# 128 more bytes of spare line between the split weights and everything allocated behind them

## The chip, the cores and the metric

The kernel runs on one core of a Trainium2 chip. The metric is the device time of one execution in microseconds, median over the runs. One execution was also recorded by the profiler; its trace gives the start and duration of every instruction.

## The reference

A two-layer decoder trunk over 256 tokens of width 1024, in float32, batch 1. Layer 0 mixes with a gated linear recurrence and stick-breaking attention, layer 1 with a diagonal state-space model (S5) and a causal softmax attention; each layer has a SwiGLU feed-forward part with 2816 hidden units. Cut to what matters here:

```python
for layer in range(2):
    h = rms_norm(x, g)
    x = x + mixer(h)                    # one input projection, two branches, one output projection
    h = rms_norm(x, g2)
    x = x + (silu(h @ w_gate) * (h @ w_up)) @ w_down
return rms_norm(x, g3)
```

Nearly all of the arithmetic is `activations @ weights` with 1024 x 1024-like float32 matrices, 186 pieces of 512 KB in all.

## The kernel before, in words

Activations stay on the chip, transposed: feature on the 128 partitions, 256 tokens along the free axis. `x` holds the residual stream as 8 blocks of 128 x 256. All weights come from one array `wall`, in the order in which they are used, as 186 pieces of 128 x 1024 floats (8 blocks of 128 x 128 each).

Every float32 operand of a large product is split in two parts that TensorE reads in its one-pass format for 4-byte numbers (float32r): a rounded high part and the rest. A weight piece arrives in a tile `raw`; ScalarE writes `hi` (a copy rounded to float32r, line 109) and VectorE writes `lo = raw - hi` (line 112 or 114). An activation is split in the same way into `xh`, `xl` (and `hh`, `hl` in the feed-forward part, `yh`, `yl`, `ah`, `al`, `syh`, `syl` in the mixers). Each 128 x 128 block of weights then costs three matmuls into the same PSUM tile: hi with xh, hi with xl, lo with xh. This is line 160 (`dense`) and line 169 (`dense2`, which alternates between two outputs). The weights are the stationary operand, 128 columns, loaded anew for every matmul; the activations are the moving operand, 256 columns streamed through the array. There is one other form, line 368 (`proj_v`): the activations are stationary there, and the weights move, 512 columns per matmul. The stick-breaking attention has 16 float32r matmuls of its own (line 463, moving `sph`/`spl`, stationary `tr_r`).

Pieces are loaded up to six ahead and split up to three ahead of their use, through pools of four `raw` tiles and of five `hi` and five `lo` tiles. The order on TensorE and on the DMA queue is the order of the program text; the other engines are ordered by a scheduler.

The pools of a partition's memory are laid out one behind the other in the order in which they are opened (lines 70 to 79). A small helper puts spare space between two of them: `half_line(name)` opens a pool that holds one tile of 16 floats, 64 bytes, per unit of `n`; nothing reads or writes that tile.

```python
70  def half_line(name, es=ctx, n=1):
71      es.enter_context(tc.tile_pool(name="line_" + name, bufs=1)).tile([128, 16 * n], F32, name="line_" + name)
    ...
73  rawp = ctx.enter_context(tc.tile_pool(name="raw", bufs=LOAD_AHEAD - SPLIT_AHEAD + 1))
74  half_line("a")
75  wp = ctx.enter_context(tc.tile_pool(name="wp", bufs=SPLIT_AHEAD + 2))
76  half_line("b")
77  xp = ctx.enter_context(tc.tile_pool(name="xp", bufs=1))
    ...
160 PE.matmul(ps, lhsT=w, rhs=a, start=(j == 0 and i == 0), stop=(j == n - 1 and i == 2))
    ...
368 PE.matmul(o, lhsT=a[:, k, xs], rhs=w, start=(k == 0 and i == 0), stop=(k == 7 and i == 2))
```

In the built program the `raw` tiles start at byte 24000 of a partition and at steps of 4096 from there (192 modulo 256), the `hi` and `lo` tiles at 40448 and at steps of 4096 (0 modulo 256), `x`, `xh` and `xl` at 81472, 89664 and 97856 (64 modulo 256). The blocks inside a tile begin at multiples of 512 bytes, so this remainder holds for each of them. Further half lines keep `yh`, `yl`, `ah`, `al`, `hh`, `hl`, `syh` and `syl` at 64 modulo 256 too. So at lines 160 and 169 the moving operand always starts 64 bytes above the stationary one, modulo 256; at line 368, where the two change places, it starts 64 bytes below; at line 463, where both lie behind the weights, the two remainders are equal.

Of the kernel before, what the change touches and what calls it, by code (L numbers as in the profile page):

```python
# [49 lines left out]
def trunk_kernel(  # L50
# [19 lines left out]
    def half_line(name, es=ctx, n=1):  # L70
        es.enter_context(tc.tile_pool(name="line_" + name, bufs=1)).tile([128, 16 * n], F32, name="line_" + name)
# [1 line left out]
    rawp = ctx.enter_context(tc.tile_pool(name="raw", bufs=LOAD_AHEAD - SPLIT_AHEAD + 1))  # L73
    half_line("a")
    wp = ctx.enter_context(tc.tile_pool(name="wp", bufs=SPLIT_AHEAD + 2))
    half_line("b")
    xp = ctx.enter_context(tc.tile_pool(name="xp", bufs=1))
    rp = ctx.enter_context(tc.tile_pool(name="rp", bufs=2))
    half_line("r")
# [1175 lines left out]
```

## Time and profile before

| | us |
|---|---|
| median of 3 runs | 608.91 |
| lowest, highest | 607.36, 609.07 |
| the profiled execution, as timed | 608.91 |
| its span, first to last instruction | 607.1 |
| TensorE busy | 591.0 |
| VectorE busy | 438.4 |
| ScalarE busy | 346.2 |
| GpSimd busy | 208.3 |

The profiled execution's time equals the median, and lies 1.8 us above its span. In the trace a matmul's record begins when its operands start to stream and ends when its last result is written, so records of successive matmuls overlap, and busy time says little about pace: the pace of TensorE is the distance between the starts of two successive matmuls. A weight load has records of its own (PEld), which run beside the matmul before it. Engines are called PE (TensorE), DVE (VectorE), ACT (ScalarE), POOL (GpSimd) and SP (the queue that issues most DMAs).

### The profile page before, as it was taken

How to read it: one execution, taken by the hardware profiler on the slowest of the kernel's cores; microseconds unless marked ns; L12 is line 12 of the kernel's file. 1: busy time of each engine (PE TensorE's matmuls, PEld its weight loads, DVE VectorE, ACT ScalarE, POOL GpSimd, SP SyncE). 2: the span in 40 equal slices, each digit the busy share in tenths (PEclk: the TensorE clock that was granted, in tenths of full speed). 3: DMA queues.
4: the chain of work that ended last, by engine and by line, in shares of the span. 5: the costliest groups of instructions: out<-in, count | busy, mean ns of one | idle time of the engine just before them, and what ended most of it. 6: DMA issues, size and time to landing. Idle time of an engine off the chain costs nothing.

```text
span 607.1 us, 11926 instructions
## 1 busy us (share of the span) xinstructions
PE 591.0 (97%) x4840; PEld 576.0 (95%) x4840; DVE 438.4 (72%) x636; ACT 346.2 (57%) x480; POOL 208.3 (34%) x203
## 2 busy tenths in 40 slices
PE   8899999999999999999999999999999999999995
PEld 7799889999899999999999998899999999999994
DVE  5798998896999976637857992797756655556632
ACT  6769996942443535465656268766545434344452
POOL 0810001539999999159810000022121110021131
PEclk9999999999999999999999999999999999999998
DMA  8746345753465774536544422455555555655501
GB/s 314 257 155 194 108 161 183 243 153 128 144 198 181 240 226 156 174 105 201 181 162 128 143 91 70 167 177 189 177 194 177 189 190 181 201 174 186 196 1 70
DMA packets 29319, 102.76 MB, mean 169 GB/s; under 512 B 3520, under 2 KB 3536, under 8 KB 29264
## 3 DMA queue, kind: packets, MB, share of 16 engines
q1 hardware_dynamic: 28080, 99.36, 50.0%
q10 hardware_dynamic: 864, 1.57, 0.7%
q0 software_dynamic: 320, 1.06, 0.5%
q8 instruction: 38, 0.62, 0.4%
q14 instruction: 17, 0.14, 0.1%
HBM read 100.93 MB, written 1.05 MB: 168 GB/s over the span
## 4 chain that ended last, share of the span: by engine, by line
PE 73%; DVE 12%; ACT 6%; POOL 3%; issue 3%; DMA 2%; SPq 0%; DVEq 0%; POOLq 0%; ACTq 0%
PE mm L160 64%; DVE lo L112 3%; PE mm L169 3%; ACT u L907 1%; ACT hi L109 1%; DMA raw<-wall 1%; DMA x<-xT 1%; PE ax L169 1%; PE ax L780 1%; POOL acc L217 1%; PE mm L903 1%; PE ax L852 1%; ACT s5tt L785 1%; POOL s5st L715 1%; PE ax L260 1%
## 5 line engine op out<-in xcount | busy, mean ns | idle before, releaser
L112 DVE TENSOR_TENSOR lo<-raw,hi 128x1024 fp32r<-128x1024 f32 x184 | 245.2, 1339 | 95.4 <-ACT hi L109 95.2
L109 ACT ACTIVATE hi<-raw 128x1024 fp32r<-128x1024 f32 (+1 forms) x188 | 195.2, 1048 | 179.7 <-PE mm L160 104.9
L160 PE MATMUL mm<-xh,hi 128*128 128x256 f32 x896 | 254.6, 284 | 0.8 <-ACT xh L943 0.7
L160 PE MATMUL mm<-xh,lo 128*128 128x256 f32 x896 | 250.5, 280 | 2.2 <-DVE lo L112 2.2
L160 PE MATMUL mm<-xl,hi 128*128 128x256 f32 x896 | 250.6, 280 | 0.2
L160 PEld LDWEIGHTS mm<-xh,lo 128*128 128x128 f32 x896 | 167.8, 187 | 3.0 <-DVE lo L112 3.0
L160 PEld LDWEIGHTS mm<-xh,hi 128*128 128x128 f32 x896 | 168.4, 188 | 1.7 <-ACT xh L943 1.2
L160 PEld LDWEIGHTS mm<-xl,hi 128*128 128x128 f32 x896 | 168.3, 188 | 0.9 <-DVE xl L944 0.8
L160 PE MATMUL mm<-hl,hi 128*128 128x256 f32 x312 | 87.3, 280 | 0.0
L160 PE MATMUL mm<-hh,hi 128*128 128x256 f32 x312 | 87.2, 280 | 0.0
L160 PE MATMUL mm<-hh,lo 128*128 128x256 f32 x312 | 87.1, 279 | 0.0
L215 POOL TENSOR_TENSOR acc<-sq 128x256 f32<-128x256 f32 x5 | 4.9, 987 | 185.0 <-ACT sq L211 185.0
L304 POOL TENSOR_TENSOR t<-t,rstd 128x512 f32<-128x512 f32 x11 | 18.9, 1722 | 132.7 <-ACT t L303 132.7
L160 PEld LDWEIGHTS mm<-hh,hi 128*128 128x128 f32 x312 | 58.6, 188 | 0.0
L160 PEld LDWEIGHTS mm<-hl,hi 128*128 128x128 f32 x312 | 58.5, 187 | 0.0
L160 PEld LDWEIGHTS mm<-hh,lo 128*128 128x128 f32 x312 | 58.4, 187 | 0.0
L217 POOL TENSOR_TENSOR acc<-acc,sq 128x256 f32<-128x256 f32 x29 | 27.6, 950 | 24.5 <-ACT sq L211 23.3
L311 ACT ACTIVATE hh<-h 128x512 fp32r<-128x512 f32 x22 | 13.7, 622 | 25.5 <-DVE h L308 25.5
L326 DVE TENSOR_TENSOR x<-x,mm 128x256 f32<-128x256 f32 x32 | 13.3, 416 | 18.8 <-PE mm L160 16.2
L303 ACT ACTIVATE t<-t 128x512 f32<-128x512 f32 x22 | 13.7, 622 | 17.0 <-DVE t L302 16.6
L227 DVE SCALAR_TENSOR_TENSOR xl<-x,vec,xh 128x256 fp32r<-128x256 f32 x32 | 21.8, 698 | 2.0 <-ACT xh L225 1.9
L308 DVE TENSOR_TENSOR h<-mm,t 128x512 f32<-128x512 f32 x22 | 15.1, 688 | 10.6 <-PE mm L160 8.4
(333 smaller groups left out, 982.1 us busy)
## 6 DMA issues: line engine op xcount, KB each, us to landing
raw<-wall SPq DMA_DIRECT2D x184, 512.0 KB, 3.5
raw<-wall ACTq DMA_DIRECT2D x4, 256.0 KB, 5.4
x<-xT SPq DMA_DIRECT2D x4, 256.0 KB, 5.1
gw<-gates SPq DMA_DIRECT2D x1, 512.0 KB, 7.2
p_b<-bst POOLq DMA_DIRECT2D x1, 512.0 KB, 4.1
p_c<-cst POOLq DMA_DIRECT2D x1, 512.0 KB, 4.8
outT<-x SPq DMA_DIRECT2D x2, 256.0 KB, 2.5
outT<-x ACTq DMA_DIRECT2D x2, 256.0 KB, 2.5
```

The costliest lines, as they stand in the source:

```text
L109: last_hi[0] = S.activation(out=hi[p][:, cs], in_=raw[p][:, cs], func=AF.Copy)
L112: i = V.tensor_sub(lo[p][:, cs], raw[p][:, cs], hi[p][:, cs])
L160: PE.matmul(ps, lhsT=w, rhs=a, start=(j == 0 and i == 0), stop=(j == n - 1 and i == 2))
L169: PE.matmul(pss[i], lhsT=w, rhs=a, start=(j == 0 and not begun), stop=(j == 2 and i not in [o for o, _ in order[n + 1:]]))
L217: acc_t[1] = G.tensor_add(out=acc_t[0], in0=acc_t[0], in1=sq[:, k, :])
L227: i = eng.scalar_tensor_tensor(out=xl[:, k, :], in0=x[:, k, :], scalar=gk, in1=xh[:, k, :], op0=ALU.mult, op1=ALU.subtract)
L260: PE.matmul(ps[:, j * 128:(j + 1) * 128], lhsT=y[:, j:j + 1].to_broadcast([128, 128]), rhs=ident, start=True, stop=True)
L303: S.activation(out=t, in_=t, func=AF.Silu)
L304: R.tensor_mul(t, t, bc(r[0], 2))
L308: V.tensor_mul(h, pu, t)
L311: S.activation(out=hh, in_=h, func=AF.Copy)
L326: V.tensor_add(x[:, k, :], x[:, k, :], pd)
```

## The change

```diff
     wp = ctx.enter_context(tc.tile_pool(name="wp", bufs=SPLIT_AHEAD + 2))
-    half_line("b")
+    half_line("b", n=3)
     xp = ctx.enter_context(tc.tile_pool(name="xp", bufs=1))
```

The spare space behind the weights grows from 64 to 192 bytes. In the built program every tile that is allocated behind it, thus all activations, the S5 tables and the attention tiles, starts 128 bytes higher than before; `raw`, `hi`, `lo` and the small constants stay where they were. `xh` goes from 89664 to 89792, which is 192 modulo 256, and so do all the other split activations. At lines 160 and 169 the moving operand then starts 192 bytes above, or 64 bytes below, the stationary one modulo 256; at line 368 it starts 64 bytes above it. Between two tiles that both lie behind the weights nothing changes. No instruction is added, removed or moved: on each engine the same instructions stand in the same order.

## The prediction

> **What bounds the kernel now.** I read the page's busy times first, then the chain of work that ended last, then the chain in order of time, and then single starts in the timeline, since the change can act only on how fast an instruction runs.
>
> ```profile
> span 607.1 us, 11926 instructions
> PE 591.0 (97%) x4840; PEld 576.0 (95%) x4840; DVE 438.4 (72%) x636; ACT 346.2 (57%) x480; POOL 208.3 (34%) x203
> ...
> PE 73%; DVE 12%; ACT 6%; POOL 3%; issue 3%; DMA 2%; SPq 0%; DVEq 0%; POOLq 0%; ACTq 0%
> ```
>
> TensorE is busy for 97% of the span, and 73% of the chain is TensorE. Two groups of the list of waits say which way the dependence runs (columns: total us, number of waits, longest):
>
> ```profile
> ACT hi L109 <- PE mm L160: 104.9, 62, 3.5
> ...
> PE mm L160 <- DVE lo L112: 2.2, 4, 0.7
> ```
>
> The engine that splits the weights waits 104.9 us for matmuls to give buffers back; matmuls wait 2.2 us for the split. So the matmuls of lines 160 and 169 set the pace. The table of windows, taken over the whole execution for each of these two lines, counts them (length, PE busy, count, clock, DMA share, GB/s; line 160 first):
>
> ```profile
> 0.00:607.00 607.00, 481.61 (x3960) 1.00 0.52 169
> 0.00:607.00 607.00, 38.56 (x312) 1.00 0.52 169
> ```
>
> That is 4272 matmuls of 256 columns, each with its own weight load. Their pace, from two pieces of the chain in order of time (start, length, what):
>
> ```profile
> 28.82 11.31 PE mm L160 x96
> ...
> 421.72 146.99 PE mm L160 x1248
> ```
>
> 11.31 us over 96 is 117.8 ns, 146.99 us over 1248 is 117.8 ns: the same number to a tenth, 400 us apart, whichever activations move. 4272 times 117.8 ns is 503 us of the 607. One nanosecond per matmul is 4.27 us, 0.7% of the kernel, so the whole question is whether this pace depends on the offset between the two operands.
>
> **The pace has a second value, at the same offset.** In the timeline (start, duration, what) two stretches run faster:
>
> ```profile
> 13.74 0.28 PE L160 MATMUL mm<-xh,hi 128*128 128x256 f32 x1
> ...
> 19.07 0.38 PE L160 MATMUL mm<-xh,lo 128*128 128x256 f32 x1
> ```
>
> ```profile
> 344.20 0.28 PE L160 MATMUL mm<-xl,hi 128*128 128x256 f32 x1
> ...
> 349.53 0.39 PE L368 MATMUL mm<-hi,xh 128*128 128x512 f32 x1
> ```
>
> From 13.74 to 19.07 are 47 steps: 5.33 us over 47 is 113.4 ns. From 344.20 to 349.53 are 47 steps again, and 113.4 ns. The tiles are the same `hi`, `lo`, `xh`, `xl` with the moving one 64 bytes above. So at one and the same offset the stream runs at 113.4 or at 117.8 ns and stays there. It is neither the clock nor the DMA load, by the windows of the two fast stretches (columns as above):
>
> ```profile
> 13.75:18.95 5.20, 5.20 (x47) 1.00 1.03 410
> 344.30:349.40 5.10, 5.10 (x47) 1.00 0.43 143
> ```
>
> The clock is full in both, and the DMA moves 410 GB/s in one and 143 in the other. What chooses the value is not visible; the 4.4 ns between them are the trace's only price for a step of pace, and I use it below.
>
> **The change, part by part.** Nothing is added, removed or moved on any engine or queue. The addresses of everything behind the weights rise by 128 bytes. Three groups of instructions read one operand that moved and one that did not.
>
> First, the 4272 matmuls of lines 160 and 169, from 64 above to 64 below. No row of before shows 256 columns moving below. The nearest row is line 368, which has the operands the other way round and so already runs with the moving one 64 below, at 512 columns:
>
> ```profile
> 70.19 0.40 PE L368 MATMUL mm<-hi,xh 128*128 128x512 f32 x1
> ...
> 75.32 0.40 PE L368 MATMUL mm<-lo,xh 128*128 128x512 f32 x1
> ```
>
> 22 steps in 5.13 us, 233.2 ns each, with one weight load of 128 columns per matmul as at line 160. If the offset were costly, this stream would be out of line with the other. It isn't: 233.2 less 117.8 is 115.4 ns for 256 more columns, and 117.8 less 115.4 leaves 2.4 ns fixed. The time goes with the columns, as it would if the cost lay in the stream itself and not in the meeting of a stream with a load. The change of form in the attention supports this:
>
> ```profile
> 78.50 0.28 PE L160 MATMUL mm<-yh,lo 128*128 128x256 f32 x1
> 78.61 0.40 PE L463 MATMUL ax<-sph,tr_r 128*128 128x512 f32 x1
> ...
> 80.02 0.40 PE L463 MATMUL ax<-sph,tr_r 128*128 128x512 f32 x1
> 80.25 0.40 PE L463 MATMUL ax<-spl,tr_r 128*128 128x512 f32 x1
> 80.48 0.28 PE L160 MATMUL mm<-yh,hi 128*128 128x256 f32 x1
> ```
>
> While the matmul at 78.50 streams, the load of `tr_r` beside it has the same remainder as the stream, not 64 less; the step is 0.11 us as ever. While `spl` streams at 80.25 the load beside it is `hi`, 64 below: 0.23 us, as with equal remainders at 80.02 and as at line 368 with the stream 64 below. Equal, above and below show one pace per column. Two single steps at a resolution of 10 ns are weak evidence each, and a locked stream may need several matmuls to change, so this carries the forecast but not certainty.
>
> The bounds of this term, for want of the row itself: above, two steps of 4.4 ns per matmul (the stream at 64 above is known at zero and one step over its fast value, and a worse offset could add as much again or twice that); below, one step down to 113.4 ns, the fastest stretch seen. In us: 4272 times 8.8 ns is +37.6, times 4.4 ns is +18.8; downward some 150 matmuls run at 113.4 already (the 94 above and a few short pieces, an estimate), so 4120 times 4.4 is -18.1. I take 0, by the row of line 368.
>
> The Trainium skill, "TensorE: Matmul & The Clock Gate", Part 2, step 1 of the step-by-step, says that TensorE has two independent SBUF read ports, one for the moving operand and one for the weight load, and that loading the next weights takes no read bandwidth from the running matmul; by that no offset can matter and this term is 0. The same page, Back-to-back issue gap, gives 256/2.4 + 2.5 = 109.2 ns for such a step; by it the 4272 steps would take 37 us less than the trace shows. The measurement decides, the streams here stall for 4 to 9 ns that this rule has no place for, and so I don't let the page exclude the rivals below.
>
> Second, the 96 matmuls of line 368, now with the moving operand above. By the same reasoning 0; if the offset had the price of a step, 96 times 4.4 ns is 0.4 us either way, under what can be measured.
>
> Third, VectorE, ScalarE and GpSimd operations with one operand among the constants, and the DMAs into and out of moved tiles. None writes or reads `hi`, `lo` or `raw` together with a moved tile, so the split of the weights, the only large work there, keeps its addresses. What is left has slack, by the window of the last long stretch (length, then busy time of PE, PEld, DVE, ACT and POOL with counts, clock, DMA share, GB/s):
>
> ```profile
> 430.00:590.00 160.00, 160.00 (x1361) 160.00 (x1361) 93.19 (x99) 72.38 (x84) 21.47 (x14) 1.00 0.54 173
> ```
>
> Sum: 0 against the profiled execution's 608.9 us (607.1 of span and 1.8 around it), which is also the median of the runs shown.
>
> **The rivals.** Slower: the read of the next weights and the stream get in each other's way, and with the stream 64 below its later columns run into the load where they ran ahead of it before. One mechanism, at lines 160 and 169, and it decides from 0.43 ns per matmul on (1.8 us over 4272). At one step the time is 608.9 + 18.8 = 627.7; at two, 646.5. For it: there is a stall with two locked values, which is what two periodic readers of one memory would give, and the offset is what sets where they meet. Line 368 can also be read for it, if its excess belongs to its one load rather than to its 512 columns: 233.2 less twice 113.4 is 6.4 ns there against 4.4 at line 160. Against it: the single steps above, and that with equal remainders line 463 is no slower than line 368. Nothing would hide it, since PE has no gap in that window.
>
> Faster: the new offset lets the streams settle at 113.4 ns. All of them: 608.9 - 18.1 = 590.8. The rest would keep up: DVE has 160.00 less 93.19 us free in the window above, and its DMA share is 0.54, so the gain would reach the end. For it: this pace exists with these tiles. Against it: it exists at the old offset, so the offset is not what selects it, and most of the 4272 were never there. A weaker form is that only one long stretch settles differently; the piece of 1248 alone is 1248 times 4.4 ns, 5.5 us, which gives 603.4.
>
> That the change does nothing to the addresses is excluded by the built program. That the memory repeats every 128 bytes, so that 64 above and 64 below are one case, would give the forecast's time.
>
> **How the numbers follow.** A measurement of this kernel tells 0.3% (1.8 us) from no change. No dependence on the sign of the offset: 0.40, 608.9 us, its own range 607 to 611. Slower by about one step, in all or most matmuls: 0.22, around 628; slower by about two: 0.14, up to 647. Faster in all streams: 0.14, around 591; faster in part: 0.10, 597 to 607. So faster 0.24, same 0.40, slower 0.36. The range from 590 to 630 leaves out the two-step case and the tails.
>
> **What will show it.** The chain's long piece of line 160 near 420 us keeps 146.99 us over 1248, or each matmul has its new pace there; 113.4 ns would show the faster rival, 122.2 or 126.6 the slower one. The pace of line 368 near 70 us tests the relation by itself: if it falls well below 233 ns with the stream now above, the offset matters. The weight loads keep their count and the waits of ACT for PE their size, unless the pace moves. The forecast is wrong if successive starts of line 160 differ by over 0.4 ns from 117.8 in the long stretches, or if the share of them at the fast value changes.

## The result, and the profile after

The changed kernel takes 602.12 us, median of 20 runs (599.96 to 609.96), against 609.38 us for the kernel before on the same chip (20 runs, 607.36 to 610.53). The ratio is 0.9894, 95% interval 0.9869 to 0.9919: 1.1% faster. In a later set of 12 runs it had a median of 601.17 us, ratio 0.9865 (0.9843 to 0.9887).

The spread is part of the result. One of these 32 runs, of 646 us at a granted clock of 0.85, is disturbed and left out, as is one of 722 us in an experiment below, and the ratios here and below leave out every run over 1.5% above the fastest of its kernel, three of the upper times here among them (with those three the two ratios would be 0.990 and 0.989). Of the other 31 runs, 24 lie between 597.8 and 603.4 us, 7 between 606.9 and 610.0, and none between. The 20 runs of the kernel before lie within 3.2 us. The first trace of the changed kernel happens to be of a run of the upper group, 608.8 us. Its page:

```profile
span 607.0 us, 11926 instructions
PE 588.6 (97%) x4840; PEld 572.9 (94%) x4840; DVE 438.6 (72%) x636; ACT 346.0 (57%) x480; POOL 208.1 (34%) x203
...
PE 69%; DVE 12%; ACT 9%; issue 3%; POOL 3%; DMA 3%; SPq 0%; DVEq 0%; ACTq 0%; POOLq 0%
```

The instruction counts are those of before and the busy times nearly so. A matmul's record ends where the profiler puts it by a model, and is 0.28 us long at either pace, so busy time can't show the pace; all paces here are distances between successive starts. What changed shows in the chain in order of time (start, length, what). Two pieces of before that answer to pieces after:

```profile
237.82 22.82 PE mm L160 x192
...
382.06 27.38 PE mm L160 x230
```

The same pieces, and the long one near 420 us, in the first trace after:

```profile
238.76 21.97 PE mm L160 x192
...
382.45 26.63 PE mm L160 x230
...
421.57 146.99 PE mm L160 x1248
```

21.97 us over 192 is 114.4 ns where before had 118.9; the long piece is as before, 117.8 ns. A second trace of the same kernel, of a run of 603.4 us:

```profile
span 601.6 us, 11926 instructions
...
238.12 21.97 PE mm L160 x192
...
422.36 141.45 PE mm L160 x1248
```

Here the long piece takes 141.45 us, 113.3 ns a step, 5.54 us less than the 146.99 of before. Taken over the whole last stretch, 1486 steps between 422 and 597 us, this is 6.6 us, most of the 7.8 us between the medians of the two groups of times. The other traces with this offset at every step agree: among the kernels of the experiments below, the last stretch is fast in runs of 599.6 and 599.7 us and slow in one of 608.2 us. So the changed kernel has the same two paces as the kernel before, and more of its stretches run at the faster one, not the same ones in the two traces. Counted from the distance between successive starts, 113 or 114 ns were 4% of the 256-column steps before (165 of 4145), 23% in the first trace after (934 of 4137) and 62% in the second (2567 of 4113).

Line 368, whose offset the change turned the other way, changed too. In the first trace after:

```profile
67.62 0.40 PE L368 MATMUL mm<-lo,xh 128*128 128x512 f32 x1
...
75.41 0.40 PE L368 MATMUL mm<-hi,xl 128*128 128x512 f32 x1
```

34 steps in 7.79 us are 229.2 ns each, against 233.2 before.

### The profile page after: what moved, and what is told of

It reads as the page before. It is cut to its first block, busy times and chain, and to the rows that moved or that the text cites. A ratio compares the mean times of both kernels' runs of the same rounds, so it can differ in the third digit from the quotient of the medians.

```text
span 607.0 us, 11926 instructions
## 1 busy us (share of the span) xinstructions
PE 588.6 (97%) x4840; PEld 572.9 (94%) x4840; DVE 438.6 (72%) x636; ACT 346.0 (57%) x480; POOL 208.1 (34%) x203
## 4 chain that ended last, share of the span: by engine, by line
PE 69%; DVE 12%; ACT 9%; issue 3%; POOL 3%; DMA 3%; SPq 0%; DVEq 0%; ACTq 0%; POOLq 0%
PE mm L160 61%; DVE lo L112 4%; PE mm L169 3%; ACT hi L109 2%; DMA raw<-wall 2%; ACT u L907 1%; PE ax L169 1%; PE ax L780 1%; DMA x<-xT 1%; POOL acc L217 1%; PE mm L903 1%; PE ax L852 1%; DVE xc L407 1%; ACT s5tt L785 1%; POOL s5st L715 1%
```

## The experiments

"Offset" is the start of the moving operand less that of the stationary one at lines 160 and 169, modulo 256: 64 before, 192 after. The share of fast steps is counted as above. The diffs are against the kernel before unless they say otherwise.

**The changed kernel once more**

> The changed kernel once more, unchanged, for more traces of it. Theory (the offset between moving and stationary operand sets how often a stretch of matmuls locks on to the pace of 113.3 ns instead of 117.8): about a quarter or more of the 256-column steps at 113.3 ns in the trace, against 3% before; times in groups, near 600 to 603 us where the last stretch of some 1490 steps (421 to 597 us) is fast, near 608 where it is slow, since 1490 steps of 4.4 ns are 6.6 us. Rival (the gain sits elsewhere, in a wait or a transfer): all long stretches at 117.8 ns also in a trace of 600 us, and the missing 7 us in idle time of TensorE.

Measured: 601.17 us (12 runs), 0.9865 (0.9843 to 0.9887). 62% of the steps were fast, the last stretch among them, as shown above; the rival's picture, slow steps and less idle time, did not occur.

**Is it the offset, or the place of the activations?** Two kernels, the first with the activations where the change puts them and the offset of before, the second with the offset of the change and the activations at 64 modulo 256 as before:

```diff
+    half_line("z", n=2)
     rawp = ctx.enter_context(tc.tile_pool(name="raw", bufs=LOAD_AHEAD - SPLIT_AHEAD + 1))
```

> 128 bytes of spare space put ahead of the raw tiles, none more behind the weights: everything from raw upward rises by 128 bytes, activations lie at 192 modulo 256 as after the change, weights at 128, so the moving operand stays 64 above. Theory of the offset: as before, 608 to 610 us, under 10% of the steps at 113.3 ns. Rival (the place of the activations itself, 192 modulo 256, or their place against the constants, brings the gain): as after, a median of 600 to 604 us.

```diff
-    half_line("a")
+    half_line("a", n=3)
...
-    half_line("b")
+    half_line("b", n=3)
```

> 128 bytes more both ahead of and behind the weights: hi and lo rise by 128 bytes to 128 modulo 256, activations rise by 256 and stay at 64 modulo 256 as before; the moving operand is 64 below the weights. Theory of the offset: as after, a median of 600 to 604 us with times in groups, a quarter or more of the steps at 113.3 ns. Rival (the place of the activations itself): as before, 608 to 610 us.

Measured: 609.03 us for the first, ratio 1.0009 (0.9994 to 1.0025), 7% of the steps fast; 600.97 us for the second, ratio 0.9891 (0.9853 to 0.9929), 66% fast. The chain's long piece in the two (the line number of the first is one higher by the added line):

```profile
422.28 146.99 PE mm L161 x1248
```

```profile
419.08 141.46 PE mm L160 x1248
```

Moving the activations without the offset changes nothing that these runs can tell (at most 0.25%), and the offset without moving them modulo 256 brings the whole gain. The first kernel's trace also has one stretch at the fast pace with the offset of 64:

```profile
237.89 21.96 PE mm L161 x192
```

That is 114.4 ns a step, where the same piece of before had 118.9. So 64 does not exclude the fast pace.

**Is 256 bytes the period?**

```diff
-    half_line("b")
+    half_line("b", n=5)
```

> Five half lines behind the weights: the moving operand 320 above, which is 64 above modulo 256 but 64 below modulo 384 or 192 below modulo 512. Theory with a period of 256 bytes: as before, 608 to 610 us. If the period is longer (512 or more) or any shift against the old layout redraws which stretches are fast: another time, such as 600 to 605 us.

Measured: 609.01 us, ratio 1.0001 (0.9985 to 1.0016), 2% fast. 320 bytes act as 64 do. With 64 and 192 unlike, a period of 128 is out as well.

**At the start of a stretch, or at every step?** Two kernels that move only half of the tiles; the first:

```diff
-    half_line("b")
+    half_line("b", n=3)
...
-    half_line("r")
+    half_line("r", n=3)
```

> Only x, xh and xl lie 64 below the weights; 128 bytes more behind the norm tiles bring all that follows (hh, hl, yh, yl, ah, al, syh, syl) back to 64 above. In the last stretch (from 422 us) streams of xh and of hh follow each other without a gap. Theory 1 (the offset decides only when a stretch begins, and the pace is then kept): the last stretch, which begins with xh, has one pace throughout, 113.3 ns in most runs, hh included; median 600 to 604 us as after. Theory 2 (the offset acts on every step): within the last stretch xh steps at 113.3 and hh steps at 117.8 ns, about 1060 fast and 420 slow, so some 4.7 of the 6.6 us and a median near 604 us.

The second changes only `half_line("r")`, to `n=3`.

> The other half: x, xh and xl stay 64 above the weights, and what lies behind the norm tiles goes to 64 below. Theory 1 (the offset decides when a stretch begins): stretches that begin with xh stay slow, the last one at 117.8 ns throughout; 607 to 610 us, and 113.3 ns at most where yh or syh or a similar tile begins. Theory 2 (it acts on every step): the hh steps, some 420 in the last stretch and 520 in the first feed-forward part, go to 113.3 ns; 604 to 607 us.

Measured: 603.74 us for the first, ratio 0.9915 (0.9896 to 0.9934); 606.75 us for the second, ratio 0.9969 (0.9952 to 0.9987). Both are the second theory's, though the expectations had the split of the last stretch wrong, 1060 steps to 420. In the last stretch of the first kernel 956 xh steps were fast and all 528 hh steps slow; in that of the second 522 hh steps fast and 961 xh steps slow. The timeline of the first kernel where xh (offset 192) hands over to hh (offset 64), and where hh hands back (start, duration, what):

```profile
485.34 0.28 PE L160 MATMUL mm<-xh,lo 128*128 128x256 f32 x1
485.45 0.28 PE L160 MATMUL mm<-xh,hi 128*128 128x256 f32 x1
485.56 0.28 PE L160 MATMUL mm<-xl,hi 128*128 128x256 f32 x1
485.68 0.28 PE L160 MATMUL mm<-xh,lo 128*128 128x256 f32 x1
485.79 0.28 PE L160 MATMUL mm<-hh,hi 128*128 128x256 f32 x1
485.91 0.28 PE L160 MATMUL mm<-hl,hi 128*128 128x256 f32 x1
486.03 0.28 PE L160 MATMUL mm<-hh,lo 128*128 128x256 f32 x1
486.14 0.28 PE L160 MATMUL mm<-hh,hi 128*128 128x256 f32 x1
```

```profile
519.59 0.28 PE L160 MATMUL mm<-hh,lo 128*128 128x256 f32 x1
519.71 0.28 PE L160 MATMUL mm<-xh,hi 128*128 128x256 f32 x1
519.83 0.28 PE L160 MATMUL mm<-xl,hi 128*128 128x256 f32 x1
519.94 0.28 PE L160 MATMUL mm<-xh,lo 128*128 128x256 f32 x1
520.06 0.28 PE L160 MATMUL mm<-xh,hi 128*128 128x256 f32 x1
520.17 0.28 PE L160 MATMUL mm<-xl,hi 128*128 128x256 f32 x1
520.28 0.28 PE L160 MATMUL mm<-xh,lo 128*128 128x256 f32 x1
```

The three distances before 485.68 are 0.11, 0.11 and 0.12 us; from 485.79 on, with the load 64 bytes off the other way, they are 0.12, 0.12, 0.11 us, which in nanoseconds are 119, 117 and 118. On the way back they fall within four steps: 117, 117, 116, 114, then 113 and so on. So the pace is no property of the whole stretch. Where a fast stream passes to 64 here it is back at 117.8 ns at once; at 192 it can settle at 113.3 and then stays there as long as nothing interrupts. Of the 12 places in the two traces where a stream passed without a gap from 64 to 192, 8 went to the fast pace.

**The other offsets**

```diff
-    half_line("b")
+    half_line("b", n=2)
```

> Two half lines: the moving operand 128 above the weights modulo 256. No row bears on it. If the fast pace becomes likelier the further the stream starts from just ahead of the load (64 above), 128 lies between: 600 to 609 us, 10 to 60% of the steps at 113.3 ns. Rival (each offset has its own pace, and 113.3 and 117.8 are only two of them): most steps at a third value outside 113 to 118 ns, and a time outside 590 to 610 us.

The next has `n=4`.

> Four half lines: moving and stationary operand at the same remainder modulo 256, as in the attention's matmuls with tr_r. If stream and load of equal remainder meet most, the pace is 117.8 ns or worse in all stretches: 609 us or more (one step more, 122.2 ns, would give 627). Rival (equal remainders are harmless, as the single steps next to tr_r in the trace of before suggested): 600 to 610 us and no value but 113.3 and 117.8.

Two more replace `half_line("b")` by the same tile with 40 and with 56 floats, 160 and 224 bytes.

> 160 bytes of spare line behind the weights instead of 64 or 192: moving operand 160 above, or 96 below, modulo 256. Measured so far: 0 gave 120.0 ns per step, 64 gave 117.8, 128 gave 118.7 to 120, 192 gave 117.8 or 113.3. If the offset acts in steps of 64 bytes: like 128 or like 192, so 612 to 616 us or 598 to 609. If it acts more finely, a value between, around 116 to 118.5 ns per step, 602 to 612 us.

> 224 bytes: moving operand 224 above, or 32 below, modulo 256. If the offset acts in steps of 64 bytes: like 192 (598 to 609 us, 113.3 or 117.8 ns) or like 0 (616 us, 120 ns). If it acts more finely, between the two: 604 to 614 us. A pace under 113.3 ns in long stretches, with a time under 597 us, would show that no offset tried so far is the best.

The long piece of the chain near 420 us in the four, in the order 0, 128, 160, 224:

```profile
427.48 149.75 PE mm L160 x1248
```

```profile
423.51 149.76 PE mm L160 x1248
```

```profile
422.85 146.43 PE mm L160 x1248
```

```profile
422.88 147.67 PE mm L160 x1248
```

| offset | ns per step, as seen in stretches of over 100 steps | time, us | ratio to before, 95% interval |
|---|---|---|---|
| 0 | 120.0 | 617.16 | 1.0134 (1.0113 to 1.0156) |
| 64 (before) | 117.8, once 113.3 | 609.4 | |
| 128 | 118.7 or 120.0 | 614.20 | 1.0089 (1.0066 to 1.0112) |
| 160 | 117.3 or 118.7 | 610.86 | 1.0023 (1.0006 to 1.0039) |
| 192 (after) | 113.3 or 117.8 | 602.1 | 0.9894 (0.9869 to 0.9919) |
| 224 | 118.3 | 612.09 | 1.0035 (1.0022 to 1.0048) |

At 128 the theory, a part of the steps at 113.3 ns, missed, and its rival came true: a third pace, and a time over 610 us. At 0 the theory was right that the pace is no better than 117.8 ns, and its price of one step, 122.2 ns, was too high; the rival, that equal remainders are harmless, is out for 256 columns. Line 368, at 512 columns, orders the offsets otherwise. In the kernel with offset 0 (start, duration, what):

```profile
70.27 0.39 PE L368 MATMUL mm<-lo,xh 128*128 128x512 f32 x1
...
75.94 0.39 PE L368 MATMUL mm<-hi,xl 128*128 128x512 f32 x1
```

25 steps in 5.67 us are 226.8 ns each, less than 229.2 after and 233.2 before: the offset that is worst at line 160 is the best of these three at line 368. 160 and 224 lie between their neighbours in time, so steps of 64 bytes are refuted, and neither beats 192. In time, no offset tried is better than the one that the change takes.

**Can the fast pace be forced?** Against the changed kernel, with `kick_t` a constant tile at 64 modulo 256:

```diff
+    half_line("k", n=3)
+    kick_t = ctx.enter_context(tc.tile_pool(name="kick", bufs=1)).tile([128, 2, 128], F32R, name="kick_t")
+    half_line("l")
...
+    def kick():
+        ps = axt()
+        for _ in range(3):
+            PE.matmul(ps[:, 0:T], lhsT=hi[blk[0] // 8][:, 0:128], rhs=kick_t.rearrange("p a b -> p (a b)"), start=True, stop=True)
...
             first = j == 0
+            if j == 1 or (half and j == 4):
+                kick()
```

> The changed kernel, with three extra matmuls at three places (ahead of the second pair of each feed-forward part, and of the fifth pair of the first): stationary a block of hi, moving a constant tile at 64 modulo 256, thus 64 above, result unused. In the runs with only half of the tiles moved, a stream that passed from 64 above to 64 below without a gap went to 113.3 ns within four steps at 9 of 12 places. Theory (the pace at 64 below is chosen by the phase at which the stream enters, and a few steps at 64 above set it): the stretches behind the three places, some 290, 300 and 1490 steps, run at 113.3 ns in nearly all runs; times lose the group at 607 to 610 us, median 597 to 601 us although the nine matmuls cost 1.1 us. Rival (chance of the whole execution, set elsewhere): three groups of times as after, about a quarter at 607 us or more.

The control has `xh[:, 0, :]` as moving operand instead.

> The same three times three extra matmuls, but with a block of xh moving, 64 below like its neighbours. Theory (it takes steps at another offset, not an interruption): as after plus 1.1 us, three groups of times, median 601 to 605 us, the stretches behind fast in some runs and slow in others. Rival (any longer lead-in of matmuls does it): as the kernel with the extra steps 64 above, 597 to 601 us.

The count in the first expectation was wrong: 8 and not 9 of the 12 places went to the fast pace. The experiment missed. With the extra steps at 64 the median is 607.52 us (11 runs, 599.64 to 609.17; 9 of them over 605), ratio 0.9940 (0.9911 to 0.9969); with those at 192 it is 606.56 us (9 runs, 599.92 to 609.65), ratio 0.9904 (0.9868 to 0.9940). Neither removed the upper group of times. It is rather more frequent than without the extra steps (9 of 11 runs and 5 of 9 over 605 us, against 7 of 31); why is open. In the one trace of the first, two of its three places show both outcomes:

```profile
118.56 0.60 PE L274 MATMUL ax<-kick_t,hi 128*128 128x256 f32 x3
119.00 0.28 PE L163 MATMUL mm<-xh,hi 128*128 128x256 f32 x1
119.11 0.28 PE L163 MATMUL mm<-xl,hi 128*128 128x256 f32 x1
119.23 0.28 PE L163 MATMUL mm<-xh,lo 128*128 128x256 f32 x1
119.35 0.28 PE L163 MATMUL mm<-xh,hi 128*128 128x256 f32 x1
...
418.46 0.60 PE L274 MATMUL ax<-kick_t,hi 128*128 128x256 f32 x3
418.90 0.28 PE L163 MATMUL mm<-xh,hi 128*128 128x256 f32 x1
419.02 0.28 PE L163 MATMUL mm<-xl,hi 128*128 128x256 f32 x1
419.13 0.28 PE L163 MATMUL mm<-xh,lo 128*128 128x256 f32 x1
419.25 0.28 PE L163 MATMUL mm<-xh,hi 128*128 128x256 f32 x1
```

At 119 us the second step after the extra ones took 114 ns, the third 120, and the pace then stayed at 117.8; at 419 us the steps fell to 113.3 and stayed. Three steps may not be enough for the stream to settle, since it enters them after a gap; this is a guess, and longer runs of extra steps weren't tried.

## Why the prediction was right or wrong

**The number held, the mechanism did not.** The time lies inside the stated range because that range, 590 to 630, was wide enough for both signs. The forecast rested on no dependence on the offset, with 608.9 us and its own range of 607 to 611, and 602.1 us is outside that. Two signs of error that the prediction named came: line 368 fell from 233.2 to 229.2 ns, and the share of fast steps rose. That the total came so near is luck, since how many stretches would run fast was no part of the forecast.

**Right: what the time hangs on.** Lines 160 and 169 set the pace, the two paces of 113.4 and 117.8 ns are real and stable, and their distance is the right price for this offset. It was the term that could move the kernel, and it did.

**Wrong: "I take 0, by the row of line 368."** The step read a price per column out of two streams that differ in columns and in offset at once, and took the agreement (2.4 ns fixed, the rest with the columns) as a sign that the offset does nothing. The prediction named the test itself, and it went against it: with the offset turned, line 368 runs at 229.2 instead of 233.2 ns. The offset had a price there all along, which the difference in columns hid. Read the other way, the row would have misled too: at line 368 the offset of 192 is the slower of the two, at line 160 the one that can be fast. So no row of before held the sign.

**Wrong: the single steps beside `tr_r`.** They showed equal remainders at the usual pace. With equal remainders throughout, the pace at 256 columns is 120.0 ns, and at 512 columns, the form of those steps, it is 226.8 ns once settled: slower than usual in the one form, faster in the other. The traces of the split kernels show why one step says nothing: after a change of offset the pace takes up to four steps to settle. The prediction had that reservation and leaned on the steps all the same.

**Wrong: "it exists at the old offset, so the offset is not what selects it."** The offset does not select the pace alone, but it sets how often a stretch gets there: 2 to 7% of the steps at 64 (one trace each of three kernels), 23 to 66% at 192 (two traces of the changed kernel and one of that with the weights moved). That a state exists under both settings says nothing about how often it occurs under each. So the rival with one long stretch at the faster pace, given 0.10 and 603.4 us, is what happened, mostly; its sum, 1248 times 4.4 ns or 5.5 us, was measured as 146.99 less 141.45, or 5.54 us. The forecast of no change, 608.9 us, was 6.8 us too high.

**The slower rival** had the wrong sign at this offset. Offsets that cost exist, 0 and 128, at up to 2.2 ns per step, half of the step that I had priced. Whether its mechanism, the stream running into the load, is the one at work is not shown.

**Half right: that the gain reaches the end.** In the last stretch it does, to the last tenth; behind it the second trace loses 0.4 us, where its clock falls earlier than in the trace of before. Ahead of it most is given back. The first trace after has 769 more fast steps than before (934 less 165), worth 3.4 us at 4.4 ns, and a span only 0.1 us shorter. Three waits of TensorE in its timeline, which the same stretch of before does not have:

```profile
66.42 0.71 PE L448 MATMUL ax<-qk 64*128 64x256 f32 x4 [0.70 <-DVE qk L527]
...
85.60 0.50 PE L463 MATMUL ax<-spl,tr_r 128*128 128x512 f32 x1 [0.75 <-DVE spl L492]
...
90.06 0.66 PE L473 MATMUL ax<-e,vt 128*64 128x256 f32 x4 [0.37 <-DVE z L465]
```

1.8 us go there, in the attention, where the wait is for VectorE and not for the stream; the rest of the 3.3 us is spread over many places, none of them over 0.3 us. The second trace has 918 more fast steps than before ahead of its last stretch, worth 4.0 us, and yet begins that stretch 0.64 us later. So in these two traces the last stretch alone decides what the kernel gains; the kernel with the weights moved begins it 2.6 us earlier than before, so this is no rule. That I looked for slack only in a window of the feed-forward part is why this was missed.

**Open.** What in the memory or in TensorE makes two streams at 192 bytes settle in one of two paces, and what at the entry decides between them, the runs don't show. The Trainium skill, "TensorE: Matmul & The Clock Gate", Part 2, step 1, has the weight load and the moving operand on independent read ports that take nothing from each other. The measurements decide against the second half of that for this form: the same instructions, with only the offset between the two operands changed, run at 113.3 to 120.0 ns. The 109.2 ns that the prediction took from the same page's Back-to-back issue gap is given there for an isolated matmul and not for a stream with a weight load each; no term of the sum used it.

## What to carry to other kernels

In this kernel, whose matmuls of 4-byte operands follow each other with a weight load each, the distance between the two operands' addresses modulo 256 moved the pace by up to 6%, from 113.3 to 120.0 ns. Where a kernel is built alike it costs a line to scan. The scan should cover all offsets, since neither sign nor distance alone orders them, and the form that carries the time, since 256 and 512 columns ordered them differently here. A kernel whose time falls into groups should be judged by many runs and several traces, since one trace shows one group. And a comparison of two rows that differ in two things proves neither.

## What the runs showed of the hardware that was not expected

A stream that arrives early can wait long enough for the clock to fall. In the second trace of the changed kernel, TensorE, arriving early at 151.6 us, waited for the split of a weight piece, and came back at half its clock. The wait, then steps after it, from the timeline:

```profile
153.80 0.58 PE L160 MATMUL mm<-xh,lo 128*128 128x256 f32 x1 [1.96 <-DVE lo L112]
...
154.39 0.41 PE L160 MATMUL mm<-xl,hi 128*128 128x256 f32 x1
154.60 0.41 PE L160 MATMUL mm<-xh,lo 128*128 128x256 f32 x1
```

and the clock by windows before, in and after it (length, busy time of PE, PEld, DVE, ACT and POOL with counts, clock, DMA share, GB/s):

```profile
150.00:154.00 4.00, 2.04 (x18) 1.84 (x17) 3.72 (x5) 1.79 (x3) 3.84 (x5) 0.98 0.20 78
154.00:158.00 4.00, 4.00 (x22) 4.00 (x23) 4.00 (x4) 0.73 (x1) 3.84 (x3) 0.59 0.42 131
158.00:162.00 4.00, 4.00 (x36) 4.00 (x35) 4.00 (x4) 2.53 (x3) 3.92 (x3) 1.00 0.76 258
```

Steps of 213 ns and a clock of 0.59 in the window from 154 to 158 us, full again after it: here the clock fell behind an idle time of 1.96 us. The trace of before has two shorter waits at this place, of 0.65 and 0.60 us, and a full clock; the kernel with only xh at 192, whose stretch ahead of it is fast too, has one of 2.08 us and the same fall. In the second trace of the changed kernel a lead of 1.3 us over before, at 145 us, so became a lag of 0.4 us at 162 us.

A second fall came near 383 us, and that one does not hang on the pace: the kernels with 64 throughout that were traced in the experiments (spare space ahead of `raw`, and 320 bytes) and the one with offset 0 have it too, at 381, 383 and 386 us, among slow steps. The one with 320 bytes (columns as above):

```profile
383.20:386.50 3.30, 3.30 (x18) 3.30 (x17) 3.11 (x5) 3.10 (x5) 0.00 (x0) 0.50 0.27 74
```

The fall in the second trace of the changed kernel lasts 3.4 us, from 153.83 to 157.24 us, at a clock of 0.50, so it costs about 1.7 us (an estimate from these two numbers). In the lower group of times, the 15 runs with a mean granted clock of 0.994 or more have a median of 600.1 us, the 9 with less one of 602.2, so falls of the clock are probably what parts them. The Trainium skill, "TensorE: Matmul & The Clock Gate", Part 1, gives a free-running window of about 3.4 us and half clock after an idle one; the second trace of the changed kernel agrees with the half clock, and its idle time of 1.96 us was shorter than that window.
